# Attention's 64-row products in both array halves at once, on two-bank tiles

## The chip, the cores and the metric

The kernel runs on one core of a Trainium2 chip. The metric is the device time of one execution in microseconds. Before the change the median of three runs is 669.47 us (667.94 to 669.58).

A core has TensorE (matrix products, with a separate path that loads the stationary operand; PE and PEld in the profile), VectorE (DVE), ScalarE (ACT), GpSimd (POOL), and SyncE (SP), which here issues nearly all transfers. Products land in PSUM, eight banks of 512 float32 columns on 128 partitions. Each engine works its own list of instructions in order.

## The reference

One layer of a hybrid attention step over 128 context tokens and 1024 latent tokens of width 1024. After a modulated RMS norm, one projection gives queries, keys, values and gates of two mixers. Mixer A attends globally, mixer B within 128 positions, with a learned sink logit per head. Each has 8 query heads and 2 key heads of 64 dimensions.

```
q_a, k_a, v_a, g_a, q_b, k_b, v_b, g_b = project(h, w_in, ...)     # rmsnorm of q and k per head, rotary positions
o_a = softmax(q_a . [cached k, latent k] / 8) . [cached v, latent v]           # all 1152 keys
o_b = softmax over [sink, cached keys, latent keys with |i - j| <= 128] . v    # the sink has no value
x   = x + gate * (concat(o_a * silu(g_a), o_b * silu(g_b)) @ w_out)
```

Context tokens use the same weights and attend to themselves alone. Everything is float32. The kernel keeps that precision by writing each operand x as a rounded high part plus the low part that is left (x = hi + lo), and multiplying hi.hi, hi.lo and lo.hi.

## The kernel before, in words

Up to about 300 us the kernel normalises, projects and writes queries (high part in 64 rows, low part in the next 64) and gates to DRAM; keys and values stay on the core. The change leaves this part nearly as it is. The rest is attention.

**Units and pairs.** A unit is one query tile of 128 tokens, one mixer and one key head, so four query heads: 512 columns, head after head. There are 36: tiles 1 to 8 of latent tokens with four units each (A and B for key head 0, A and B for key head 1), then the context tile. Two units, an A and a B, form a pair; there are 18. An A unit has 9 blocks of 128 keys, a B unit 4 (3 at the first and last tile), a context unit 1.

**Maxima** (`max_steps`, `pmx`). To find each query's largest score, A multiplies each head's queries with 3 x 384 keys, 12 products a unit (L1111), each reduced on VectorE (L1124). B multiplies each head with its window, 4 products (L1114); VectorE adds the mask and takes the maximum with the sink in one custom instruction (L1129). The queries stand as high and low parts in 128 rows against the key's high part twice, so one product sums both. The negated maxima are transposed (L1168), copied on ScalarE (L1179), sent to DRAM (L1180), and come back as one row of the tile `qb` (L1184).

**Scores** (`score_steps`, `st`). For each block two products of 512 columns go into one bank: the key's high part against high and low queries (L1371, 128 rows), and 65 rows of the key's low part with a row of ones against the high queries and the row of negated maxima (L1372). At a B window's edges VectorE adds the mask (L1377). ScalarE takes the exponential into a `pe` tile (L1383). The `pe` tiles of a unit are added up (L1396): A's eight adds on GpSimd, B's three on VectorE.

**Burst** (`values`, `pv`). At the due time `v2` of a pair TensorE multiplies all `pe` tiles with the values, two products a block, one in each half of the output partitions (L1413); behind each unit's blocks come the products of the sum `acc` with ones, which give the softmax's denominator. Each is recorded as two matmuls. Then the ends: `t` adds the sink's weight (B, VectorE), `e` inverts by a logarithm and an exponential (ScalarE), `g` multiplies (VectorE), `o` applies the gate (GpSimd), `h` and `l` split into high and low parts (ScalarE, GpSimd).

**Output projection** (`out_items`, `po`). Each pair adds 24 products of 512 columns to its tile's two banks (L1488); when the tile's second pair is in, VectorE multiplies by the gate and adds the residual (L1495, L1496), and SP stores.

**Order.** Every step has a due time in the tables `STEPS` and `OTHER`, given per pair and shifted by `PAIR = 13` for each next one; LATE gives those of 24 gate products left over from the projection. `of_pair` posts the steps, and the loop at the end emits them by due time. `in_order` then ties each engine, SP too, to that order, so an engine never works ahead past a step that waits.

PSUM tiles: two banks A for maxima, two B for scores, two C for bursts, D and E for the output.

## Time and profile before

| What | us |
|---|---|
| Median of three runs (lowest, highest) | 669.47 (667.94, 669.58) |
| Span of the profiled execution | 667.9 |
| TensorE, its weight loads busy | 659.0, 519.3 |
| VectorE, ScalarE, GpSimd busy | 438.8, 281.6, 333.1 |
| Transfers | 81.41 MB, mean 122 GB/s |

The page gives no time for the profiled execution other than its span; the lowest run lies at 667.94, the median 1.6 above the span. A matmul's own duration in the groups, some 395 ns for 512 columns, includes its way through the array; how closely they follow one another is read from the chain, which gives each its share of time.

### The profile page before, as it was taken

What the parts mean: (1) busy time and instruction counts of PE and PEld (TensorE: products, weight loads), DVE (VectorE), ACT (ScalarE), POOL (GpSimd) and SP (SyncE); (2) the same over time, 40 slices, a digit from 0 to 9 for tenths busy, and PEclk for the clock granted to TensorE, in tenths of its full rate; (3) what the DMA queues carried; (4) which work ended last, traced back from release to release, by engine and by line L of the source; (5) the groups of instructions that cost most, each with busy time, mean ns of one, the idle gap of its engine ahead of it and who ended that gap; (6) DMA issues with size and microseconds to landing.
All of it is one profiled execution on the core that took longest, in us unless ns stands there. A gap on an engine that the chain in (4) does not pass through costs nothing.

```text
span 667.9 us, 10668 instructions
## 1 busy us (share of the span) xinstructions
PE 659.0 (99%) x3767; PEld 519.3 (78%) x3767; DVE 438.8 (66%) x923; ACT 281.6 (42%) x586; POOL 333.1 (50%) x325
## 2 busy tenths in 40 slices
PE   8999999999999999999999999999999999999997
PEld 3789988877788788997777777777777777777766
DVE  3566147786674866446768878688787786875533
ACT  4545411242141453435554355444454355434531
POOL 3457013332321332357885575657665675557712
PEclk9999999999999999999999999999999999999999
DMA  9970365437645310734142303223132212332233
GB/s 357 414 261 14 131 224 158 87 78 225 184 111 142 95 48 33 228 128 146 58 132 99 100 26 102 88 72 92 45 119 88 71 51 86 123 93 77 75 104 111
DMA packets 55837, 81.41 MB, mean 122 GB/s; under 512 B 7388, under 2 KB 26932, under 8 KB 54760
## 3 DMA queue, kind: packets, MB, share of 16 engines
q1 hardware_dynamic: 47464, 68.97, 30.8%
q10 hardware_dynamic: 8320, 11.77, 7.0%
q8 instruction: 30, 0.49, 0.3%
q14 instruction: 23, 0.19, 0.1%
HBM read 61.42 MB, written 19.29 MB: 121 GB/s over the span
## 4 chain that ended last, share of the span: by engine, by line
PE 92%; DVE 2%; ACT 2%; DMA 1%; issue 1%; ACTq 1%; POOL 0%; DVEq 0%
PE pv L1413 15%; PE po L1488 15%; PE st L1371 7%; PE st L1372 7%; PE pmx L1111 5%; PE pq L482 4%; PE pq L483 4%; PE pq L481 4%; PE pg L496 3%; PE pg L491 3%; PE pg L495 3%; PE pk L482 2%; PE pk L483 2%; PE pk L481 2%; PE pmx L1114 2%; PE px L645 1%
## 5 line engine op out<-in xcount | busy, mean ns | idle before, releaser
L1396 POOL TENSOR_TENSOR acc<-acc,pe 128x512 f32<-128x512 f32 x112 | 150.2, 1341 | 6.8 <-ACT pe L1383 0.6
L1383 ACT ACTIVATE pe<-st 128x512 f32<-128x512 f32 x208 | 120.6, 595 | 65.0 <-PE st L1372 52.2
L1124 DVE TENSOR_REDUCE mx<-pmx 128x1 f32<-128x384 f32 x192 | 104.5, 554 | 35.0 <-PE pmx L1111 32.2
L1413 PE MATMUL pv<-pe,v_all 128*64 128x256 f32 x832 | 96.8, 381 | 0.0
L1413 PEld LDWEIGHTS pv<-pe,v_all 128*64 128x64 f32 x832 | 58.2, 137 | 33.0 <-PE st L1372 4.2
L1488 PE MATMUL po<-wo,ogh 128*128 128x512 f32 (+1 forms) x224 | 79.3, 386 | 0.0
L399 POOL TENSOR_TENSOR rs_q<-ms_q,mhalf 128x8 f32<-128x8 f32 x18 | 34.8, 1932 | 80.4 <-DVE ms_q L397 80.4
L1111 PE MATMUL pmx<-kha,qt 128*128 128x384 f32 x192 | 64.2, 347 | 0.0
L1371 PE MATMUL st<-qt,kha 128*128 128x512 f32 x144 | 57.4, 399 | 0.5 <-ACT pe L1383 0.5
L1372 PE MATMUL st<-qb,kla 65*128 65x512 f32 x144 | 57.2, 397 | 0.0
L1129 DVE CUSTOM_DVE_ANT_0 pmx<-pmx,mask,nsink 128x512 f32<-128x512 f32 (+1 forms) x64 | 44.2, 722 | 11.3 <-PE pmx L1114 11.2
L1488 PEld LDWEIGHTS po<-wo,ogh 128*128 128x128 f32 x224 | 41.5, 189 | 9.6 <-ACT ogh L1450 0.6
L1445 POOL TENSOR_TENSOR spare<-spare,sgl 128x256 f32<-128x256 f32 x27 | 19.6, 737 | 49.9 <-DVE spare L1441 47.5
L1111 PEld LDWEIGHTS pmx<-kha,qt 128*128 128x128 f32 x192 | 35.3, 189 | 11.4 <-issue 5.0
L1488 PE MATMUL po<-wo,ogl 128*128 128x512 f32 (+1 forms) x112 | 43.2, 387 | 0.0
L664 POOL TENSOR_TENSOR h<-hf,h 128x256 fp32r<-128x256 f32 (+2 forms) x33 | 28.0, 863 | 21.3 <-DVE h L663 21.2
L1396 DVE TENSOR_TENSOR acc<-acc,pe 128x512 f32<-128x512 f32 x28 | 34.3, 1224 | 5.2 <-ACT pe L1383 3.9
L842 ACT ACTIVATE sqq<-pq 128x512 f32<-128x512 f32 x18 | 10.8, 600 | 53.3 <-DMA qd<-qo0q 15.2
L1371 PEld LDWEIGHTS st<-qt,kha 128*128 128x128 f32 x144 | 27.1, 189 | 5.6 <-ACT pe L1383 1.2
L495 PE MATMUL pg<-h,whigb 128*128 128x512 f32 (+2 forms) x88 | 30.0, 341 | 0.0
L1372 PEld LDWEIGHTS st<-qb,kla 65*128 65x128 f32 x144 | 27.0, 188 | 3.6
L496 PE MATMUL pg<-h,wlogb 128*128 128x512 f32 (+2 forms) x88 | 29.7, 337 | 0.0
(236 smaller groups left out, 1502.6 us busy)
## 6 DMA issues: line engine op xcount, KB each, us to landing
qt<-qd SPq DMA_DIRECT2D x36, 256.0 KB
wm<-in_w_mod_ss_dram SPq DMA_DIRECT2D x8, 1024.0 KB
qd<-qo0q ACTq DMA_DIRECT2D x36, 128.0 KB
qd<-qo1q ACTq DMA_DIRECT2D x36, 128.0 KB
qb<-qd SPq DMA_DIRECT2D x36, 128.0 KB
sgl<-gd SPq DMA_DIRECT2D x36, 128.0 KB
out_dram<-yt SPq DMA_DIRECT2D x17, 256.0 KB
wg<-in_w_mod_g_dram SPq DMA_DIRECT2D x4, 1024.0 KB
```

The costliest lines, as they stand in the source:

```text
L481: nc.tensor.matmul(out, h_at(0, i, k, tok), w.hi[k], start=(k == 0), stop=False)
L495: nc.tensor.matmul(out, w.hi[k][:, cs], h_at(0, i, k, to), start=(k == 0 and first), stop=False)
L496: nc.tensor.matmul(out, w.lo[k][:, cs], h_at(0, i, k, to), start=False, stop=False)
L1111: nc.tensor.matmul(pm[:, 0:384], lhs, kha[:, g, 3 * b : 3 * b + 3, :], start=True, stop=True)
L1124: nc.vector.tensor_reduce(mx[:, h, b : b + 1], pm[:, 0:384], axis=AX.X, op=ALU.max)
L1129: nc.vector.tensor_tensor_reduce(s, s, mask[:, m0 : m0 + P * (p1_ - p0)], -1.0, nsink[:, 4 * g + h : 4 * g + h + 1], op0=ALU.add, op1=ALU.min,
L1371: nc.tensor.matmul(s, kh, qtile[i], start=True, stop=False)
L1372: nc.tensor.matmul(s, kl, qbtile[i], start=False, stop=True)
L1383: nc.scalar.activation(pe, v["s"], AF.Exp)
L1396: (nc.vector if (m, b) in ADD_DVE else nc.gpsimd).tensor_tensor(acc[i], first, pe, op=ALU.add)
L1413: nc.tensor.matmul(pv[HD * s : HD * s + HD, o : o + 256].rearrange("p (c n) -> p c n", c=2), lhs, r[:, :, s, :], start=start, stop=stop)
L1488: nc.tensor.matmul(po[c], x, wo_parts[KT * n + k][lo][:, q], start=(k == KS[0] and p == 0), stop=(k == KS[-1] and p == 2))
```

## The change

The attention's TensorE work, bursts apart, is cut into products of 64 contraction rows. They are issued two by two: one uses rows 0 to 63 of the array, the other rows 64 to 127, and they write to two different banks.

- Queries are loaded so that the high part stands in both halves of `qt`, the low part in both halves of `qb` (`twice`, two transfers for each). The row of maxima is broadcast to 128 partitions, a tile `nm` of its own; a constant tile `part` of -1/64 turns it into "minus the maximum" by a product. Keys' low parts have 128 rows.
- Maxima take the high parts alone, two heads at once: an A unit has four pairs of products of 512 columns and two of 128, reduced from two banks in five reduces; a B unit has two pairs and two reduces. For B, ScalarE writes the mask into PSUM first and the products add to it. The first pair's two A units (`early`) keep their 12 products.
- Scores are made for two key blocks at once in a two-bank tile, four products in each half: hi.hi, hi.lo, lo.hi and the maxima. At a window's edges ScalarE writes the mask first. One exponential takes both banks. A's ninth block is cut by heads, 256 columns in each half.
- The output projection multiplies 64 rows at a time, one half into each of the tile's two banks, and the halves swapped for 12 of a pair's 24 steps; the context tile's keeps 128 rows.
- PSUM becomes two tiles S of two banks (scores and part of the maxima), one tile C of two banks (both units' burst, the other maxima), D and E. A's maxima use S, C, S, C, C; B's use C, C.
- The burst holds both units' values; a plain product among them transposes the next pair's maxima. The products with ones stand behind both units' values, as a step `vs`.
- Of B's three adds the first two move to GpSimd (`ADD_DVE`).
- All due times are new: `STEPS` for even pairs, `ODD` for odd ones, `OTHER` for seven pairs.

The order that the new due times give on TensorE around a burst, in two neighbouring pairs in the middle: burst, ones-products, 4 or 7 output products, one or two of B's score groups, B's first maximum, then output products, A's score groups and maxima by turns, with the last A group shortly ahead of the next burst. GpSimd's order is: the two gatings `o`, B's adds (in every second pair one of them among A's), the low parts `l`, and A's eight adds.

```diff
+PE2 = 7
+PE1 = 2
...
-ADD_DVE = ((1, 1), (1, 2), (1, 3))
+QBS = 2
+ADD_DVE = ((1, 3),)
...
+TURN_AT = 4
+MAX_AT = ("SCSCC", "CC")
+PRE = ()
...
-    kla = kv.tile([65, 2, 9, P], F32R, name="kla")
+    kla = kv.tile([P, 2, 9, P], F32R, name="kla")
...
+    part = kv.tile([P, P], F32R, name="part")
+    nc.vector.tensor_scalar(part.rearrange("p (a n) -> p a n", a=2), ones.unsqueeze(1).to_broadcast([P, 2, HD]),
+                            -1.0 / HD, None, op0=ALU.mult)
...
+    def twice(to, src):
+        for s in range(2):
+            nc.sync.dma_start(to[HD * s : HD * s + HD].bitcast(F32), src)
+
+    HALF = (slice(0, HD), slice(HD, P))
...
-        nc.sync.dma_start(qt_.bitcast(F32), q_dram[t][m][:, 512 * g : 512 * g + 512])
+        twice(qt_, q_dram[t][m][0:HD, 512 * g : 512 * g + 512])
...
+        def masked(k):
+            p0, p1_ = cut(k)
+            v[k] = pair_of_banks(MAX_AT[1][k], f"pmx{i}_{k}")
...
+            nc.scalar.copy(v[k][:, :, 0:w], mask[:, m0 : m0 + w].unsqueeze(1).to_broadcast([P, 2, w]))
...
+                p0, p1_ = cut(k)
+                w = P * (p1_ - p0)
+                if m == 0:
+                    v[k] = pair_of_banks(MAX_AT[0][k], f"pmx{i}_{k}")
+                for a, h in enumerate((k,) if m else (0, 1) if k == 4 else (k // 2,)):
+                    for s, half in enumerate(HALF):
+                        at = P * (2 * h + s)
+                        nc.tensor.matmul(v[k][:, s, w * a : w * a + w], q[half, at : at + P],
+                                         (khb if m else kha)[half, g, p0:p1_, :], start=m == 0 and a == 0, stop=True,
+                                         skip_group_check=m == 1 or a > 0)
 
...
+            elif m == 0 and k == 4:
+                nc.vector.tensor_reduce(mx[:, :, 2].rearrange("p (a s) -> p s a", s=2),
+                                        pm[:, :, 0 : 2 * P].rearrange("p s (a n) -> p s a n", a=2), axis=AX.X, op=ALU.max)
...
+                h, b = divmod(k, 2)
+                nc.vector.tensor_reduce(mx[:, 2 * h : 2 * h + 2, b], pm, axis=AX.X, op=ALU.max)
...
-                nc.vector.tensor_tensor_reduce(s, s, mask[:, m0 : m0 + P * (p1_ - p0)], -1.0,
-                                               nsink[:, 4 * g + h : 4 * g + h + 1], op0=ALU.add, op1=ALU.min,
-                                               accum_out=mx[:, h : h + 1])
+                p0, p1_ = cut(k)
+                nc.vector.tensor_reduce(mx[:, 2 * k : 2 * k + 2], pm[:, :, 0 : P * (p1_ - p0)], axis=AX.X, op=ALU.max)
...
-            qb_ = qp.tile([65, 512], F32R, tag="qb", name=f"qb{i}", bufs=QBS)
-            nc.sync.dma_start(qb_[0:64, :].bitcast(F32), q_dram[t][m][0:64, 512 * g : 512 * g + 512])
+            qb_ = qp.tile([P, 512], F32R, tag="qb", name=f"qb{i}", bufs=QBS)
+            twice(qb_, q_dram[t][m][HD:P, 512 * g : 512 * g + 512])
...
-            nc.sync.dma_start(qbtile[i][64:65, :].bitcast(F32),
-                              r_dram[i // 2][4 * m : 4 * m + 4].rearrange("(o h) n -> o (h n)", o=1))
+            nmtile[i] = qp.tile([P, 512], F32R, tag="nm", name=f"nm{i}", bufs=2)
+            nc.sync.dma_start(nmtile[i].bitcast(F32),
+                              r_dram[i // 2][4 * m : 4 * m + 4].rearrange("(o h) n -> o (h n)", o=1).to_broadcast([P, 512]))
...
+    def pair_of_banks(tag, name):
+        return ps2.tile([P, 2, 512], F32, tag=tag, name=name, bufs={"S": 2, "C": 1}[tag])
...
+            def before(j=j, two=two, edge=edge, v=v):
+                v["s"] = pair_of_banks("S", f"st{i}_{j}")
...
+                if edge:
+                    x = x.rearrange("p s (h n) -> p s h n", n=P)
+                    k = mask.rearrange("p (s n) -> p s n", n=P)
+                    k = (k[:, 0::3].unsqueeze(2).to_broadcast([P, 2, 4, P]) if two else
+                         k[:, 3 if t == NL else 0].unsqueeze(1).unsqueeze(1).to_broadcast([P, 2, 2, P]))
+                    nc.scalar.copy(x, k)
...
+            def product(j=j, blks=blks, two=two, edge=edge, pre=pre, v=v):
+                assert i in rowed
+                if not pre:
+                    v["s"] = pair_of_banks("S", f"st{i}_{j}")
+                qh, ql = qtile[i], qbtile[i]
+                last = 3 if edge or not pre else 2
+                for n in range(last + 1):
+                    for s, half in enumerate(HALF):
+                        kh, kl = blks[s if two else 0][0:2]
+                        k, q = ((kh, qh), (kh, ql), (kl, qh), (part, nmtile[i]))[n]
+                        to = v["s"][:, s] if two else v["s"][:, s, 0:256]
+                        nc.tensor.matmul(to, k[half], q[half, :] if two else q[half, 256 * s : 256 * s + 256],
+                                         start=n == 0 and not pre, stop=n == last, skip_group_check=pre)
...
+            def weights(j=j, blks=blks, two=two, v=v):
+                if two:
+                    pe = w3.tile([P, 2, 512], F32, tag="pe2", name=f"pe{i}_{j}", bufs=PE2)
+                    nc.scalar.activation(pe, v["s"], AF.Exp)
+                    v["pe"] = [pe[:, 0], pe[:, 1]]
+                else:
+                    pe = w3.tile([P, 512], F32, tag="pe1", name=f"pe{i}_{j}", bufs=PE1)
+                    nc.scalar.activation(pe.rearrange("p (s n) -> p s n", s=2), v["s"][:, :, 0:256], AF.Exp)
+                    v["pe"] = [pe]
...
-        n = len(made)
-        for b, (blk, pe) in enumerate(made):
-            product(0, blk[1], pe, first and b == 0, False)
-        if not last:
-            return
-        product(256, ones, acc.pop(i), False, True)
+        for b, (lhs, pe) in enumerate(made):
+            if b == (min(at, len(made) - 1) if then else -1):
+                then()
+            product(0, lhs, pe, b == 0, False)
...
+        def halves(r, k, p):
+
+            for s, half in enumerate(HALF):
+                c = (r + s) % 2
+                first = k == KS[0] and p == 0 and r == 0
+                if first:
+                    po[c] = one_bank(pieces[c][2], f"po{t}_{c}")
+                oh, ol = (x[half, k % 2, :] for x in og[t, k // 2])
+                x, lo = ((oh, 0), (oh, 1), (ol, 0))[p]
+                nc.tensor.matmul(po[c], x, wo_parts[KT * c + k][lo][half], start=first,
+                                 stop=k == KS[-1] and p == 2 and r == 0, skip_group_check=True)
...
-        mms = [lambda c=c, k=k, p=p: mm(c, k, p) for c in range(len(pieces)) for k in ks for p in range(3)]
+        if last:
+            mms = [lambda c=c, k=k, p=p: mm(c, k, p) for c in range(len(pieces)) for k in ks for p in range(3)]
+        else:
+            mms = [lambda r=r, k=k, p=p: halves(r, k, p) for r in (g, 1 - g) for k in ks for p in range(3)]
...
+    def burst(i):
+
+        pvt = pair_of_banks("C", f"pv{i}")
+        u = i // 2 + 1
+
+        def turned():
+            if 2 * u < NU:
+                rowpt[u] = pvt[0:12, 1, 0:P]
+                nc.tensor.matmul(pvt[0:HD, 1, 0:P], m_all[u % 2].bitcast(F32), ident_r.bitcast(F32), start=True, stop=True)
+
+        values(i - 1, pvt, TURN_AT, turned)
+        if u in puts_:
+            puts_[u]()
+        values(i, pvt)
+
+    def burst_sums(i):
+
+        for j in (i - 1, i):
+            assert added.get(j, 0) == sum(len(blks) for blks, _ in held_[j]) - 1
+            sums[j]()
 ```

## Prediction

> **What bounds the kernel now.** I read the page's busy times first, then its chain, then two steady stretches of the attention part, then the chain in order of time there, and last the groups of instructions between 330 and 640 us. Engines and shares of the whole span:
>
> ```profile
> PE 659.0 (99%) x3767; PEld 519.3 (78%) x3767; DVE 438.8 (66%) x923; ACT 281.6 (42%) x586; POOL 333.1 (50%) x325
> PEclk9999999999999999999999999999999999999999
> PE 92%; DVE 2%; ACT 2%; DMA 1%; issue 1%; ACTq 1%; POOL 0%; DVEq 0%
> 375.29:396.94 21.65, 21.65 (x129) 16.49 (x131) 15.82 (x32) 10.12 (x21) 13.56 (x14) 1.00 0.21 68
> 396.94:418.59 21.65, 21.65 (x129) 16.49 (x131) 18.14 (x36) 10.11 (x21) 13.56 (x14) 1.00 0.28 92
> ```
>
> TensorE holds 92% of the chain at full clock. The last two lines are one pair of units each (PE, PEld, DVE, ACT, POOL busy us): PE is busy for all of it, VectorE for 16 to 18, GpSimd for 13.6. So TensorE's issue sets 21.65 us a pair. Its prices, from the chain in order of time (start, us, what):
>
> ```profile
> 331.36 0.35 PE pmx L1111 x2
> 332.91 6.19 PE pv L1413 x56
> 375.29 6.62 PE pv L1413 x60
> 381.91 0.54 PE pmx L1111 x2
> 382.45 1.16 PE po L1488 x5
> 383.62 0.23 PE st L1371
> 383.85 0.23 PE st L1372
> 390.72 0.24 PE st L1372
> 390.95 0.47 PE pmx L1114 x2
> 396.94 6.62 PE pv L1413 x60
> 591.61 6.62 PE pv L1413 x60
> 650.48 1.95 PE pv L1413 x16
> ```
>
> A 512-column product costs 0.235 (0.231 in `po`), a 384-column one 0.175; a burst costs 6.62 for 60, 0.110 each. Check: scores 26 x 0.235 = 6.11, maxima 12 x 0.175 + 4 x 0.235 = 3.04, burst 6.62, output 24 x 0.231 = 5.54, 0.19 for leaving the burst (0.54 against 0.35), 0.1 for a transpose: 21.6.
>
> **The change on TensorE.** Call p the price of two 64-row products, one in each array half, 512 columns. No row shows one. The nearest is the burst, whose products stand in two column halves: two cost 0.221. The other end is today's 0.235 for one full product; I take 0.228, since both the columns and today's form are kept. In such slots a pair has: A's scores 4 groups x 4 + one half-wide group = 18, B's 8, output 24, so **none of these loses a slot**; A's maxima 4 and two of 128 columns, about 4.5, instead of 12 full products; B's maxima 2 instead of 4. That is 56.5 p. Burst 6.62, leaving it 0.19, and the transpose, now a plain product inside the burst, at most one slot (0.22): 7.03 more. PE per pair: 56.5 x 0.221 + 7.03 = 19.5 to 56.5 x 0.235 + 7.03 = 20.3, so 1.3 to 2.1 less, nearly all from the maxima. The 24 late gate products keep 128 rows, in three clusters by their due times: six changes of form, 6 x 0.1 = 0.6 us once.
>
> The Trainium skill, "TensorEngine Tiling (Array Packing)", section "Tiling Modes" (Key Properties), says that changing the tiling mode drains TensorE. The 0.54 against 0.35 agrees. By this rule the output projection is cut in halves for the mode, not for speed; left at 128 rows among the scores, each of its some 10 clusters a pair would cost two drains, 10 x 0.19 = 1.9 us by the row, and the maxima's gain would be gone.
>
> **The change on the other engines.** Groups between 330 and 640 us (busy us, mean ns), and GpSimd in order of time:
>
> ```profile
> L1396 POOL TENSOR_TENSOR acc<-acc,pe 128x512 f32<-128x512 f32 x102 | 137.0, 1343 | 5.8
> L1456 POOL TENSOR_TENSOR ogl<-of,ogh 128x256 fp32r<-128x256 f32 x7 | 5.1, 733 | 3.6 <-ACT ogh L1450 3.6
> L1158 POOL TENSOR_TENSOR m_all<-m_all,sink 128x4 f32<-128x4 f32 x16 | 3.2, 203 | 21.8 <-DVE m L1150 18.2 <-DMA er<-rd 3.3
> 383.82 0.73 POOL L1445 TENSOR_TENSOR of<-of,sgl 128x256 f32<-128x256 f32 x1 [5.65 <-DVE of L1441]
> 384.51 0.74 POOL L1445 TENSOR_TENSOR spare<-spare,sgl 128x256 f32<-128x256 f32 x1
> 387.86 4.04 POOL L1396 TENSOR_TENSOR acc<-acc,pe 128x512 f32<-128x512 f32 x3
> 391.85 0.75 POOL L1456 TENSOR_TENSOR ogl<-spare,ogh 128x256 fp32r<-128x256 f32 x1
> L1383 ACT ACTIVATE pe<-st 128x512 f32<-128x512 f32 x182 | 105.6, 595 | 59.1 <-PE st L1372 46.7 <-DVE st L1377 9.5
> L1434 ACT ACTIVATE rs<-rs 128x256 f32<-128x256 f32 x30 | 12.5, 417 | 1.0
> L1433 ACT ACTIVATE rs<-rs 128x256 f32<-128x256 f32 x15 | 6.3, 418 | 25.0 <-DVE rs L1428 25.0
> L1450 ACT CAST ogh<-spare 128x256 fp32r<-128x256 f32 x22 | 8.8, 398 | 0.0
> L1244 ACT CAST wo_big<-wraw 128x512 fp32r<-128x512 f32 x1 | 0.6, 611 | 0.0
> L1124 DVE TENSOR_REDUCE mx<-pmx 128x1 f32<-128x384 f32 x156 | 84.7, 553 | 19.2 <-PE pmx L1111 16.6
> L1122 DVE TENSOR_REDUCE mx<-pmx 128x4 f32<-128x512 f32 x4 | 2.7, 680 | 0.0
> L1396 DVE TENSOR_TENSOR acc<-acc,pe 128x512 f32<-128x512 f32 x27 | 33.2, 1228 | 5.2 <-ACT pe L1383 3.9
> L1496 DVE TENSOR_TENSOR yt<-po,yt 128x512 f32<-128x512 f32 x14 | 9.7, 692 | 0.5
> L1441 DVE TENSOR_TENSOR of<-pv,rs 128x256 f32<-128x256 f32 x8 | 3.4, 425 | 3.4 <-ACT rs L1434 3.4
> L1428 DVE TENSOR_TENSOR rs<-pv,er 128x256 f32<-128x256 f32 x15 | 6.4, 424 | 6.9 <-PE pv L1413 6.9
> ```
>
> ScalarE: no row has 1024 columns. Bounds: 0.595 (no price for more columns) and 1.19 (two of today's). From 256 to 512 columns it goes from 0.40 to 0.60, so 0.2 for 256 and about 1.0 for 1024. A pair then has six exponentials at 1.0 and one at 0.6, and three masks written to PSUM at 1.0: with 1.67 for the inverses, 0.8 for casts and 0.46 of small ones 12.5, against 10.1. Room in 20.
>
> VectorE: 128 columns more cost 0.127, so a two-bank reduce about 1.2 (bounds 0.68 and 2 x 0.68). Six of them, one of 512, one add and the ends make some 12 against 16 to 18: the masks' adds, the fused mask-and-maximum and two of B's three adds go. VectorE gets room.
>
> A tile's two output banks now fill together, so their sums on VectorE (2 x 2 x 0.69 = 2.8) come at once, and the next tile's first output product waits for them. Two or three score groups stand between, 1.9 to 2.8: 0 to 0.9 every second pair, in the waits below.
>
> GpSimd gets what VectorE loses: B's first two adds. Three in a row took 4.04, 1.35 each; the eight of A are 10.8, the two of B 2.7.
>
> DMA and its queue (issue ns as least, median, most; waits in us, times, longest):
>
> ```profile
> L1135 SPq DMA_DIRECT2D qb<-qd x36: 451/476/1112, 283.0 to 642.1; - x36
> L1184 SPq DMA_DIRECT2D qb<-rd x36: 220/244/433, 287.3 to 643.1; - x36
> SPq L1180 <- ACT spare L1179: 142.1, 17, 13.1
> ```
>
> The query halves come twice and the row of maxima goes to 128 partitions: 2 x (128 + 256) KB a pair, some 37 GB/s on 68 to 92. SP issues one `qt` and one `qb` more a unit and a broader row, 2 x (2 x 0.48 + 0.24) = 2.4 us a pair. SP stood 142.1 us, 8.4 a pair, behind the copy of the transposed maxima, so there is room. That copy moves into the burst; behind its wait on SP stand the rows of maxima that the next scores need. They have the rest of the burst, about 4.9 us, for two trips through DRAM; no row here times one trip. I take it as hidden; uncovered, up to 1 us a pair.
>
> **What is late next.** The two ones-products now stand behind both units' values, and need A's last add on GpSimd. By the due times GpSimd then does: both gatings, B's two adds, both low halves, the small sink step, A's eight adds. That closes a ring, from A's last add to A's last add of the next pair:
>
> - ones-products, 8 x 0.110: 0.9
> - total, two inverse steps, multiplication: 0.424 + 0.418 + 0.417 + 0.425, and 0.3 for handing over (estimate): 2.0
> - gatings 1.43, low halves 1.45, sink step 0.2: 3.1
> - B's adds 2.7, A's adds 10.8: 13.5
> - waits for exponentials and casts. After the ends (2.0) ScalarE first writes a mask into the freed tile (1.0) and only then takes B's first exponential (1.0), ready at 4.0, while GpSimd is there at 2.0 + 1.4 = 3.4: 0.6; a cast or A's first exponential alike: 1.4 in all. Bounds 0 and 2.8.
>
> Sum 20.9; 19.5 to 22.3 with its bounds. It is longer than PE's 19.5 to 20.3, so **GpSimd's ring becomes the bound**, and of the 1.3 to 2.1 us won on TensorE 21.65 - 20.9 = 0.75 is left. It now has no such ring to close: POOL idles 8 of 21.65.
>
> From the second burst (332.91) to the fourteenth (591.61) are twelve periods: 12 x 0.75 = 9.0. Ahead of it two units keep their twelve products, B's maxima lose 8 and the stretch's VectorE work shrinks: 2 won, 0.6 lost. From the fourteenth burst to the last (650.48) are 58.9 us, four periods of 14.7: the two full ones have no more than 20.9 to lose, the prompt's little to add: 0 to 2 lost, and the last output products, still 128 rows, stay; 1 won by half the maxima. Net 10.5. Profiled span 667.9 less 10.5 is 657.4; the runs' median, 669.47, is 1.6 above that span, the lowest run equals it. Forecast: **659**.
>
> **Rivals.** *TensorE stays the bound*: the ring's waits vanish because the schedule puts other work there. For it: 19.5 is the ring's own lower end. Gain 1.3 to 2.1 over some 14 pairs, 18 to 29: about 646 (640 to 651). Chance 0.2.
>
> *Slower: the one two-bank tile C.* It carries the burst of both units, both B maxima and three of A's. Place: ahead of B's first maximum after a burst. Price: burst 6.84, ends 2.0, B's maxima 2 x (mask 1.0 + 0.23 + 1.2), A's 2 x (0.23 + 1.2) + 0.8, and a wait for TensorE's last columns, about 0.2, six times: 18.6. It decides once its seven hand-overs lose over 0.44 each, (21.65 - 18.6) / 7; at 0.55 it is 22.45, 14 x 0.8 = 11 more: 680. Against it: much of that loss is room the engines have. Chance 0.14. The same page of the Trainium skill, section "Performance Considerations" (PSUM Bottleneck), warns that tiling speeds TensorE but not PSUM evacuation; the trace of before shows no such wait.
>
> *No change*: the ring takes its upper waits, 21.6: 668 to 670. Chance 0.1.
>
> *The halves do not work side by side.* Each slot then costs 0.47, 56.5 x 0.235 = 13 more a pair, some 200: 870. Only the column halves speak against it. Chance 0.03.
>
> **How the numbers follow.** Forecast 0.53 (its own range 652 to 666), the rivals 0.2, 0.14, 0.1, 0.03. A measurement can tell some 0.3%, 2 us. Faster: 0.53 + 0.2 = 0.73; same 0.1; slower 0.17. Range 644 to 674: it leaves out the fastest of the first rival and most of the slow ones.
>
> **What would show it.** Right: periods between bursts of 20.5 to 21.2; TensorE idle ahead of the ones-products, released by POOL `acc`, some 0.5 us a pair; two products starting within 0.01 us and the next two 0.22 to 0.235 later; POOL near 17 us a pair. Wrong: idle time ahead of B's maxima released by ScalarE (tile C), periods below 20.3 with no wait on `acc`, or slots of 0.3 and more.

## The result, and the profile after

The changed kernel takes 696.98 us (median of 4 runs, 696.4 to 698.48), the kernel before 668.86 (4 runs, 667.94 to 669.58) on the same chip. The ratio is 1.0422, with a 95% interval of 1.0403 to 1.044: 28 us slower, where 659 was forecast and 674 was the upper end. The profiled execution is the slowest of the four (698.48 us), so its spans are some 1.5 us above the median run's.

The page of the profiled execution (span 696.7): busy times, TensorE's clock and the chain's engines.

```profile
PE 662.0 (95%) x4684; PEld 513.0 (74%) x4684; DVE 370.3 (53%) x653; ACT 310.2 (45%) x542; POOL 370.2 (53%) x358
PEclk9999999999999999998999999999999999999999
PE 77%; DMA 12%; ACT 4%; DVE 2%; SPq 2%; issue 1%; ACTq 1%; POOL 0%; DVEq 0%
```

TensorE held 92% of the chain before and holds 77% now; transfers went from 1% to 12%. Where the 28.8 us of span lie can be read from the bursts of value products: the second and the fourteenth, from the chain in order of time (start, us, what).

```profile
340.60 1.95 PE pv L1414 x16
606.85 1.88 PE pv L1414 x16
```

The second starts 7.7 later than before (332.91). The twelve periods to the fourteenth take 266.25 (258.70): 7.6 lost. From there to the end 89.85 (76.3): 13.5. Two pairs in the middle, as stretches (span, then PE, PEld, DVE, ACT, POOL busy):

```profile
385.24:406.97 21.73, 20.79 (x184) 15.26 (x186) 11.39 (x14) 12.77 (x20) 15.96 (x16) 1.00 0.39 117
406.97:429.62 22.65, 21.56 (x185) 15.59 (x186) 14.07 (x18) 11.55 (x18) 16.28 (x16) 1.00 0.45 135
```

In both TensorE is idle for 0.9 to 1.1 us; before it was for none. In the twelve periods this makes 12.4 us (253.83 busy of 266.25).

For the steady pairs I added up, from the starts of all matmuls in the trace, each one's time until the next starts:

| us a pair | scores | maxima | output | burst with transpose | sum |
|---|---|---|---|---|---|
| before | 6.19 | 3.26 | 5.56 | 6.63 | 21.6 |
| after | 6.84 | 1.92 | 5.86 | 7.54 | 22.2 |

The maxima won 1.3, as forecast. The rest lost 1.9, though it has no more slots but the transpose. What the losses are shows in the products' waits from 300 us on (us in all, times, longest), and in SP's from 380 to 607:

```profile
PE st L1384 <- DMA nm<-rd: 11.8, 12, 2.2
PE pv L1414 <- ACT spare L1133: 6.1, 17, 0.4
PE pmx L1067 <- DMA qt<-qd: 1.7, 6, 0.5
```

```profile
SPq L1134 <- ACT spare L1133: 58.5, 10, 7.6
```

Scores wait for the row of maxima (`nm`): 3.4 us ahead of the second burst, 5.2 in the twelve periods (7 times), 3.1 behind them; a burst's value products wait for ScalarE's copy of the transposed maxima; maxima wait for queries, which stand on SP behind the write that waits for the same copy (before, SP stood 101.1 us behind its copy in such a window, and no product waited for queries). Behind the fourteenth burst scores also wait 1.9 us for queries. GpSimd's `acc`, the bound that was forecast, is not among them. The way of the row in one pair, from the chain:

```profile
387.11 0.10 PE pv L1552
387.22 2.30 PE pv L1414 x19
...
389.54 0.26 ACT spare L1133
...
389.82 1.27 DMA rd<-spare
...
391.14 3.87 DMA nm<-rd
...
395.06 1.43 PE st L1384 x10
```

The transposing product (L1552) is done at 387.2, but the copy starts 2.3 us later, at 389.54: it is released by the last of A's value products, which write to the same tile. Then the write takes 1.3 and the load to 128 partitions 3.9. From the product's start to the first use of the row are 7.9 us. TensorE's other work fills most of them: in this pair it stands 0.36 us ahead of the value products that wait for the copy and 0.58 ahead of the product that needs the row.

### The profile page after: what moved, and what is told of

Read it like the earlier page. It is cut to its first block, busy times and chain, and to the rows that moved or that the text cites. A ratio compares the mean times of both kernels' runs of the same rounds, so it can differ in the third digit from the quotient of the medians.

```text
span 696.7 us, 12252 instructions
## 1 busy us (share of the span) xinstructions
PE 662.0 (95%) x4684; PEld 513.0 (74%) x4684; DVE 370.3 (53%) x653; ACT 310.2 (45%) x542; POOL 370.2 (53%) x358
## 4 chain that ended last, share of the span: by engine, by line
PE 77%; DMA 12%; ACT 4%; DVE 2%; SPq 2%; issue 1%; ACTq 1%; POOL 0%; DVEq 0%
PE st L1384 13%; PE pv L1414 10%; PE po L1502 10%; DMA nm<-rd 7%; PE pq L411 4%; PE pq L412 4%; PE pq L410 4%; PE pmx L1067 4%; PE pg L420 3%; PE pg L424 3%; PE pg L425 3%; DMA rd<-spare 2%; PE pk L411 2%; PE pk L412 2%; PE pk L410 2%; DMA qt<-qd 2%
## 5 line engine op out<-in xcount | busy, mean ns | idle before, releaser
L1414 PE MATMUL pv<-pe,v_all 128*64 128x256 f32 x832 | 101.1, 384 | 6.2 <-ACT spare L1133 6.1
L1390 ACT ACTIVATE pe<-st 128x1024 f32<-128x1024 f32 x92 | 92.8, 1025 | 21.0 <-PE st L1384 18.3
L1502 PE MATMUL po<-wo,ogh 64*128 64x512 f32 x384 | 97.2, 404 | 0.0
L1414 PEld LDWEIGHTS pv<-pe,v_all 128*64 128x64 f32 x832 | 64.0, 136 | 35.2 <-ACT spare L1133 13.9
L1085 DVE TENSOR_REDUCE mx<-pmx 128x2 f32<-128x1024 f32 x56 | 67.8, 1221 | 14.8 <-PE pmx L1067 14.5
L1384 PE MATMUL st<-nm,part 64*128 64x512 f32 (+1 forms) x232 | 49.0, 388 | 11.8 <-DMA nm<-rd 11.8
L1088 DVE TENSOR_REDUCE mx<-pmx 128x2 f32<-128x1024 f32 (+1 forms) x32 | 37.0, 1156 | 39.0 <-PE pmx L1067 37.6
L1502 PEld LDWEIGHTS po<-wo,ogh 64*128 64x128 f32 x384 | 50.7, 187 | 7.0 <-issue 1.9
L1502 PE MATMUL po<-wo,ogl 64*128 64x512 f32 x192 | 53.3, 396 | 0.0
L1502 PE MATMUL po<-wo_big,ogh 64*128 64x512 f32 x128 | 48.2, 412 | 0.0
L1343 POOL TENSOR_TENSOR acc<-pe 128x512 f32<-128x512 f32 x28 | 36.2, 1293 | 21.9 <-ACT pe L1390 21.8
L1384 PEld LDWEIGHTS st<-nm,part 64*128 64x128 f32 x232 | 25.5, 188 | 21.7 <-DMA nm<-rd 18.4
L1042 ACT CAST pmx<-mask 128x1024 f32<-128x1024 bf16 (+1 forms) x32 | 30.8, 963 | 12.8 <-DVE mx L1088 6.6
L1384 PE MATMUL st<-qt,kha 64*128 64x512 f32 (+1 forms) x160 | 33.8, 391 | 0.9 <-ACT pe L1394 0.4
L1067 PE MATMUL pmx<-kha,qt 64*128 64x512 f32 (+1 forms) x168 | 31.1, 357 | 2.5 <-DMA qt<-qd 1.7
L1384 PE MATMUL st<-qb,kha 64*128 64x512 f32 (+1 forms) x160 | 32.8, 376 | 0.0
```

Of the source, the lines that this page charges most:

```text
L1067: nc.tensor.matmul(v[k][:, s, w * a : w * a + w], q[half, at : at + P], (khb if m else kha)[half, g, p0:p1_, :], start=m == 0 and a == 0, ...
L1085: nc.vector.tensor_reduce(mx[:, 2 * h : 2 * h + 2, b], pm, axis=AX.X, op=ALU.max)
L1088: nc.vector.tensor_reduce(mx[:, 2 * k : 2 * k + 2], pm[:, :, 0 : P * (p1_ - p0)], axis=AX.X, op=ALU.max)
L1343: (nc.vector if (m, b) in ADD_DVE else nc.gpsimd).tensor_tensor(acc[i], first if b == 1 else acc[i], x, op=ALU.add)
L1384: nc.tensor.matmul(to, k[half], q[half, :] if two else q[half, 256 * s : 256 * s + 256], start=n == 0 and not pre, stop=n == last, skip_gr ...
L1390: nc.scalar.activation(pe, v["s"], AF.Exp)
```

## The experiments

**Is it the row, or the queries queued behind it?** Theory R: the row's way. Rival Q: SP's queue. Rival C: tile C or GpSimd's adds hold the pair anyhow.

`e1_copy_early`, the copy written down right behind the product:

```diff
-        values(i - 1, pvt, TURN_AT, turned)
-        if u in puts_:
-            puts_[u]()
+        def turned_and_put():
+            turned()
+            if u in puts_:
+                puts_[u]()
+        values(i - 1, pvt, TURN_AT, turned_and_put)
```

> One call moved: ScalarE's copy of the transposed maxima is written down right behind the transposing product, ahead of the rest of A's value products; same instructions, same queues. Theory R (the way of the row of maxima: product, copy, write, broadcast load, first scores, too long for the work that TensorE has left): in the changed kernel the copy starts 2.4 us after the product, when A's last value product signals. With the call moved it should start within 0.4 us, B's value products should lose their 0.5 us a pair, and the waits of the scores for the row (30 us in 31 waits, most of 2 us or less) should nearly go: 696.7 - 17 x 0.5 - some 20 = 668 (660 to 676). Rival Q (not the row, but the query loads queued on SP behind the write that waits for the copy): these start 2.2 us sooner too, and only the waits of the maxima for the queries go, 0.4 us a pair beside the 0.5: 681 (678 to 686). Rival C (the one tile of two banks C, or GpSimd's adds, hold the pair at 22.2): only the place of the wait changes, 693 to 697.

Measured: 686.69 (ratio to before 1.0279, 1.0255 to 1.0303), 10.3 better than the changed kernel, little more than a third of what R expected and nearer to Q's 681; the waits below and e3 decide between them. R's 30 us add the weight loads' waits for the row (18.4) to the products' (11.8), which are largely the same time twice. ScalarE's copy in order of time (start, us; last, in brackets, the idle time before it and what ended it), the products' waits from 300 us on, and the chain after a burst:

```profile
404.05 0.25 ACT L1133 COPY spare<-pv 12x128 f32<-12x128 f32 x1 [1.37 <-PE pv L1552]
```

```profile
PE pmx L1067 <- ACT pmx L1042: 7.2, 14, 0.7
PE pv L1414 <- ACT spare L1133: 6.3, 17, 0.8
PE st L1384 <- DMA nm<-rd: 1.7, 2, 1.5
```

```profile
411.97 1.03 ACT pmx L1042
412.99 0.04 issue
413.04 0.54 PE pmx L1067 x2
...
413.67 1.24 DVE mx L1088
414.91 0.02 issue
414.93 1.02 ACT pmx L1042
415.95 0.96 ACT pe L1390
416.91 0.04 issue
416.95 1.21 PE st L1384 x8
```

The copy is now released by the product itself. The waits for the row fell from 11.8 to 1.7, but two others hold: A's next value product now waits for the copy, since both touch one tile, and B's maxima wait for ScalarE's mask. That is the turn of tile C: ends, mask, product, reduce, second mask, and a score group's exponential behind it on ScalarE. Periods are 21.6 and 22.3 by turns, the shorter no better than the 21.65 of before.

`e2_two_rows`, `e3_write_on_scalar`, `e4_old_row`:

```diff
 e2:
-            nc.sync.dma_start(nmtile[i].bitcast(F32), ... .to_broadcast([P, 512]))
+            nc.sync.dma_start(nmtile[i].bitcast(F32)[0::HD], ... .to_broadcast([2, 512]))
...
+                        rows_ = half if n < 3 else slice(HD * s, HD * s + 1)
...
 e3, e4:
-            nc.sync.dma_start(r_dram[u][a:b], rw)
+            (nc.scalar if u else nc.sync).dma_start(r_dram[u][a:b], rw)
 e4:
-                              r_dram[i // 2][4 * m : 4 * m + 4]...
+                              r_dram[max(i // 2 - 1, 0)][4 * m : 4 * m + 4]...
...
-                    nc.scalar.activation(pe, v["s"], AF.Exp)
+                    nc.scalar.activation(pe, v["s"], AF.Exp, scale=0.25)
```

> The row of maxima is loaded to 2 partitions (0 and 64) instead of 128, and its product takes one contraction row in each half instead of 64; the sum is the same. Copy, write and queue are as in the changed kernel. Theory R: the load takes 3.9 us from issue to landing in the changed kernel, 128 times 2 KB; with two rows it should land in some 2 us, which takes off most of the 30 us that scores wait for the row: 680 (674 to 686), while B's value products still wait 0.5 us a pair. Rival Q: the query loads stand as late as before, 692 to 697. Rival C: 694 to 697.

> The write of the transposed maxima to DRAM is issued by ScalarE's queue, right behind its copy, instead of SP's; so SP no longer stands behind the copy, and the query loads behind it go out earlier. Rival Q: the waits of the maxima for the queries go (about 0.4 us a pair in the steady part, 14 pairs) and the start and the end of the stretch gain as much: 684 (680 to 689). Theory R: copy, write and load of the row stay as late as they are, so the waits of the scores stay: 690 to 697. Rival C: 694 to 697.

> Leaves out the dependence on the pair's own maxima: the row is loaded from the pair before (same load, same bytes, same product), the write goes out on ScalarE's queue, and the exponentials are scaled by 0.25 so that they stay finite; the output is not the reference's. Nothing then waits for the way from the transposing product to the row but the sink's weights. Theory R: the waits of the scores for the row go, those of B's value products for the copy (0.5 us a pair) stay: 674 (668 to 682). Rival C: another wait takes the place, 692 to 697. Rival Q: as in the run with the write on ScalarE, 680 to 689.

Measured: e3 695.03, 2.0 better, so Q falls: with SP free of the copy the maxima's waits for queries shrink (0.4 in one), but the row's stay (12.0 us in 9 waits). e4, which leaves out each pair's own row and so does not compute the reference, takes 683.3, 13.7 better: that much is won with the row's way gone and the write on ScalarE's queue, and then the mask's wait (7.1) and the copy's (6.1) stand as in e1. e2 722.41, 25 worse than the changed kernel, though its row came in time. The weight loads' waits of e2:

```profile
PEld st L1385 <- issue: 39.4, 112, 0.7
PEld st L1385 <- DMA nm<-rd: 1.1, 2, 0.8
```

The smaller load did what R said; but 112 times a score product now waits 0.35 us for nothing that the trace names, where the changed kernel has none of note: the one-row products stand between 64-row ones, and I take it as the price of a change of form, which g0 below bears out.

**What is left?** Theory W: two independent waits. Theory G: GpSimd's ring. `e5_turn_in_s` and its variants:

```diff
 e5, on e1:
+                tt = pair_of_banks("S", f"tt{u}")[:, 0] if u < NU // 2 - 1 else pvt[:, 1]
+        d["sa"] = d["sa"][:4] + (max(d["sa"][4], DUE[u - 1]["po"][11] - PAIR + 0.001),)
 e6, on e5:
-            nc.scalar.copy(v[k][:, :, 0:w], mask[:, m0 : m0 + w].unsqueeze(1).to_broadcast([P, 2, w]))
 e7, on e5:
+    d["nx"] = (the due time of the third output product behind it, ...)
 e8, on e5:
-ADD_DVE = ((1, 3),)
+ADD_DVE = ((1, 1), (1, 2), (1, 3))
```

> As the run with the copy moved, but the transposing product writes to a free tile S instead of B's bank of the burst's tile, so no value product shares a tile with what ScalarE copies (the last transpose of all stays where it was). So that the output products of both row halves into one bank stay ordered, the last A score group, half a group, is placed behind the neighbouring output products, ahead of the burst. Theory W (what is left after the row's way are two waits of their own: 0.56 us a pair of the value products behind the copy, and some 0.75 a pair of B's maxima for ScalarE's mask in tile C): the first goes, 17 x 0.56 = 9.5 off 686.7: 677 (673 to 681). Theory G (GpSimd's adds in a ring with the ones-products, the forecast's own bound, 20.9 a pair or a little more, hold the pair now): the wait reappears ahead of the ones-products: 683 to 687.

> As the run with the transpose in tile S, but the masks that ScalarE writes ahead of B's maxima are left out (no work in their place; the products start the banks afresh), so B's maxima also run over keys outside the window. Theory W: the wait of B's maxima for the mask, 0.75 us a pair in the run with the copy moved, goes with 2 us of ScalarE's work a pair: 677 - 14 x 0.75 = 666 (662 to 671). Theory G: the ring stays: within 3 us of the run with the transpose in tile S.

> As the run with the transpose in tile S, but B's first maximum is placed three output products later in TensorE's list in pairs 2 to 15 (three slots, 0.7 us); masks, reduces and queues stay. Theory W: the same 0.75 us a pair is then filled with output products: 667 (663 to 672), nearly as without the masks. Rival: tile C's turn (burst, ends, mask, B's first maximum, reduce, second mask) is itself the bound, so the wait only moves to B's second maximum or the next burst: 675 to 680.

> As the run with the transpose in tile S, but all three of B's adds are on VectorE again, so GpSimd has 2.6 us a pair less. Theory G: the ring loses 2 x 1.31 us, and the period falls by what the ring holds: 10 us or more faster than with the transpose in tile S, below 670. Theory W: GpSimd has 16 us of work in a pair of 22 and no ring closes: within 2 us of the run with the transpose in tile S, 675 to 680.

Measured: e5 690.45, e6 682.0, e7 694.95, e8 698.07. All four missed W's numbers, for a reason that e5's own edit brings in:

```profile
PE st L1392 <- DVE mx L1093: 9.7, 6, 1.6
```

The moved score group came behind the mask of the next pair's edge tile, got the other tile S, and waited for a reduce in every second pair (e5's periods: 21.65 and 23.1). Within the four, e6 is 8.5 below e5: the masks cost that. In e7 the steady periods are e5's to 0.1 us but for one, so nothing was filled, as its rival said; with the artefact in both, it tests no more than that. In e8 VectorE's reduces are late instead (5.2 us of waits for them), and nothing is won; e5's products wait for GpSimd's adds only once, 0.2 us, so no ring holds there.

With the edge mask behind the transpose (f2), and three versions on that: f1 lets VectorE add B's mask again, f3 is f1 with e3's write on ScalarE's queue, f4 is f2 with the edits of e6 and e3.

```diff
 f2, on e5:
+    d["pb"] = tuple(max(x, DUE[u - 1]["v2"] - PAIR + 0.0005) for x in d["pb"])
 f1, on f2, beside the mask's line of e6:
-                nc.vector.tensor_reduce(mx[:, 2 * k : 2 * k + 2], pm[...], axis=AX.X, op=ALU.max)
+                    nc.vector.tensor_tensor_reduce(pm[:, s, 0:w], pm[:, s, 0:w], mask[:, m0 : m0 + w], 1.0,
+                                                   sink[...], op0=ALU.add, op1=ALU.max, accum_out=mx[:, h : h + 1])
```

> As the run with the transpose in tile S, but the mask that ScalarE writes into a score tile S for the next pair's B edge is placed behind the burst's transpose in every pair. In that run it stood ahead of the last A score group in every second pair, so that this group got the tile whose reduce was late, and TensorE stood 2 us (every second period 23.1 instead of some 21.2). Theory T (the turn of the one tile C, burst, ends, mask, B's first maximum, reduce, second mask, is the bound once the row comes early): the artefact goes, 6 x 1.9 = 11 off 690.5, and the periods stay near 21.5: 679 (676 to 683). Theory W (tile C's waits can be filled by TensorE): 668 (664 to 672).

> As the run with the edge mask later, but B's maxima get their mask as in the kernel before: VectorE adds it and takes the maximum in one custom instruction per head (0.76 + 0.14 us), ScalarE writes no mask for them. Theory T: two masks of 1.0 leave tile C's turn and VectorE takes 2 x (2 x 0.9 - 1.2) = 1.2 more in it, and ScalarE's exponentials no longer stand behind the second mask: 0.9 to 1.3 us a pair, 14 pairs: 665 (661 to 670). Theory G (GpSimd's ring): no change against the run with the edge mask later, within 2 us.

> As the run with the fused mask, but the write of the transposed maxima is issued by ScalarE's queue. Theory R (way of the row): in the steady part nothing changes; in the last three pairs, which have little other work, the loads of the row stand on SP behind that write and behind two query loads, 2.6 us, so 2 to 4 us at the end: 662 (658 to 667). Rival (the end is bound by its products and ends): within 1 us of the run with the fused mask.

> Leaves out the masks ahead of B's maxima as in the run without them (so the maxima also run over keys outside the window), with the edge mask later and the write on ScalarE's queue. Bound of what the mask's place can give: all three waits gone. Theory T: periods of 20.5, as in the undisturbed pairs of the run without masks: 661 (657 to 665), 2 to 4 below the run with fused masks and write. Theory G: periods stay at 21 or more: 670.

Measured: f2 680.8, as T said: against e1 5.9 less, which I take as the price of the copy's tile: the waits for the copy fell from 6.3 to 0.4 (f2 also moves one score group and the edge's mask). f1 675.57 (1.0111, 1.0095 to 1.0126): 5.2 less, where some 14 were expected. f3 676.84, no gain where 662 was expected. f4, which leaves out the masks ahead of B's maxima, 672.09 (1.0053, 1.0033 to 1.0073), beyond G's 670 and far from T's 661. Stretches of f4 (two pairs, then the twelve periods from its second burst), and the first of its weight loads' waits:

```profile
420.80:441.10 20.30, 20.30 (x184) 15.91 (x182) 11.37 (x14) 10.14 (x16) 15.85 (x16) 1.00 0.35 99
441.10:462.30 21.20, 20.92 (x184) 15.63 (x182) 13.61 (x18) 10.15 (x16) 16.32 (x16) 1.00 0.46 144
337.89:587.27 249.38, 247.72 (x2182) 190.79 (x2184) 148.94 (x181) 122.82 (x194) 196.73 (x184) 1.00 0.43 125
```

```profile
PEld pv L1424 <- POOL acc L1353: 6.9, 14, 0.8
```

With the three waits gone, TensorE is busy for all of every second period, 20.3 us, and the twelve periods take 249.4 against 258.7: 9.3 won. The ones-products now wait for GpSimd's adds, as they did in f2 (8.8 us of weight loads' waits there, 16 times). In the longer period shown, from the last value product ahead of them (446.78) to the first of them it is 0.66 us instead of 0.11, so the adds make some 0.55 of the 0.9 by which the longer period exceeds the shorter. f1, which computes all of the reference, takes 253.9 for the twelve periods, 4.8 less than before, and loses 3.3 ahead of them and 7.4 behind. In f4 the second burst still comes 5.0 us later than before (337.89 against 332.91), and the rest takes 82.5 against 76.3.

**The start, the end, and the change of form.** g1 transposes the last pair's maxima a burst earlier; g2 adds to it the first write on ScalarE's queue and the first four gate loads behind the first rows; g3 adds to that a later place for the output sums; g0 is the changed kernel with 128-row output products; h1 is f4 and h2 is g2 without g1's edit, both with A's fourth add on VectorE.

```diff
 g1, on f3:
+                out += [("tt", j, lambda: (last_turn(i // 2), put(j)))]
...
 g2, on g1:
-        load_gate(i)
+        post(zero[0] - 40.0, lambda i=i: load_gate(i))
...
 g3, on g2:
+        d["ym"], d["ys"] = (-7.34, -7.36), (d["ys"][0], -7.33)
 g0, on the changed kernel:
-        if last:
+        if True:
             mms = [lambda c=c, k=k, p=p: mm(c, k, p) ...]
 h1, h2:
-ADD_DVE = ((1, 3),)
+ADD_DVE = ((1, 3), (0, 4))
```

> As the run with fused mask and write on ScalarE, but the last pair's maxima are transposed (into a tile S), copied and written right behind the burst before the last but one, and its rows are loaded as soon as the tiles are free, instead of from inside the last but one burst. Theory E (the end still pays the way of the row once in full: product at 643.3, first scores at 650.5 in the run without masks, with 3.4 us of other work): 4 to 5 us less, 672 (670 to 674). Rival: the end is bound by burst, ends and the last 45 output products; the wait only moves: 675 to 677.

> As the run with the last turn early, and at the start of the attention the first pair's maxima are written by ScalarE's queue too and the first four gate loads stand behind the first rows on SP, instead of ahead of them. Theory F (the start loses its 3 us against the kernel before because the write stands behind twelve issues on SP of half a us each, with the row's load behind it): first burst at some 312.5 instead of 315, 2 to 3 us less: 669.5 (668 to 672). Rival (landing itself, 3 us behind 1 MB of other loads, is the bound): within 1 us of the run before it.

> As the run with the front changed, but in pairs 3 to 13 the two output banks' sums (2.8 us on VectorE, every second pair) stand behind B's second fused maximum instead of ahead of it, and the next tile's first three output products behind the scores that follow. Theory V (in the run with fused masks every second period is 22.0 instead of 20.4 since B's second maximum waits 0.8 us for VectorE, and the rest for GpSimd's adds): five to six pairs lose 0.8 us less: 666 (664 to 669). Rival G (GpSimd's ring then takes it back): within 1.5 us of the run with the front changed.

> The changed kernel with its output projection left at 128 rows in all tiles: the same 24 products a pair at the same places in the list. It prices the change of the array's form: by the forecast's step some 10 clusters a pair, two changes each at 0.1 us from the row that leaves a burst (0.19 for both): 1.9 us a pair, 16 pairs: 30 us on top of 697, less what the waits for the row of maxima cover: 715 (705 to 727). Rival (a change of form costs nothing beside what the waits have already): 695 to 700.

> As the run without masks and with the write on ScalarE's queue (masks of B's maxima left out), but the fourth of A's eight adds moves from GpSimd to VectorE. Theory G (with the three waits gone, what is left in every second period, 21.2 instead of 20.3, is GpSimd's ring of the forecast: the ones-products wait for A's last add): the ring loses 1.3 us, these periods fall to some 20.4, 6 x 0.8 = 5: 667 (665 to 670), and the waits of the ones-products for the adds are gone. Rival (VectorE's add delays reduces or ends as in the run with B's adds on VectorE): 671 to 678, with waits for VectorE.

> A version that computes the whole reference: the run with the front changed, without its early last turn, and with the fourth of A's adds on VectorE. Theory G: from 675.5, five to six periods of 22.0 lose what they wait for the adds, some 0.6 each: 672 (669 to 675). Rival (VectorE, which has the fused masks here, is late in these periods): 675 to 680.

Measured: g1 679.37 (675.89 to 680.59), no gain: in f3 the scores wait only 0.4 us for rows from 380 us on, so there was next to none to win, and the moved transposing product itself waits 2.0 us for VectorE. g2 675.53 (1.0113, 1.0096 to 1.013), 3.8 below g1 but only 1.3 below f3, where 669.5 was expected; its first burst starts at 314.4, between f3's 315.1 and the expected 312.5. g3 687.95; in one pair its sums stand behind the next tile's first products and take those in place of their own, with as much work; elsewhere every second period is 23.4 to 24.9, and output products wait 11.4 us for the sums: a miss, which does not tell whether VectorE's order was a loss in g2. h1 683.87 and h2 684.31, outside all that was expected. In h1 no burst waits for GpSimd any more, but

```profile
PE pv L1424 <- DVE mx L1095: 6.1, 6, 1.1
```

VectorE's add waits for GpSimd's third, and A's last reduces stand behind it. So whether the ring alone holds f4's 21.2 stays open; that the wait for the adds is there, and that the two moves of work off GpSimd (e8, h1) cost more elsewhere, is shown. No version beats the kernel before.

g0 took 745.42 (1.1157, 1.113 to 1.1183): 48 more than the changed kernel. Of its weight loads' waits from 300 to 697 us, one that is 0.4 us, once, in the changed kernel, whose output projection keeps 128 rows for the context tile alone:

```profile
PEld po L1490 <- issue: 33.4, 105, 0.7
```

On the way back, score products wait 19.8 us in 61 such waits (1.3 in 4 in the changed kernel). A steady pair takes 25.4 instead of 22.2; with 17.6 changes between output and 64-row products in it, 0.18 us each.

## Why the prediction was wrong, step by step

- **Slots and p: right.** All three kinds of products run side by side. Two halves start together and the next two 0.23 later, from TensorE in order of time (x2 stands for two products):

```profile
400.97 0.40 PE L1384 MATMUL st<-qt,kha 64*128 64x512 f32 x2
401.21 0.40 PE L1384 MATMUL st<-qb,kha 64*128 64x512 f32 x2
```

p is 0.233, near the upper bound of 0.235 and not the 0.228 taken. PE is 20.3 where nothing waits (f4), the upper bound too.

- **Prices on the other engines: right.** Exponential, reduce and mask, from the groups of the page (count, busy us, mean ns):

```profile
L1390 ACT ACTIVATE pe<-st 128x1024 f32<-128x1024 f32 x92 | 92.8, 1025 | 21.0 <-PE st L1384 18.3
L1085 DVE TENSOR_REDUCE mx<-pmx 128x2 f32<-128x1024 f32 x56 | 67.8, 1221 | 14.8 <-PE pmx L1067 14.5
L1042 ACT CAST pmx<-mask 128x1024 f32<-128x1024 bf16 (+1 forms) x32 | 30.8, 963 | 12.8 <-DVE mx L1088 6.6
```

- **"I take it as hidden; uncovered, up to 1 us a pair": this is the step that failed.** The step put the term at nothing, judging the row's way by two transfers against 4.9 us. The copy begins 2.3 us late, since it is released by A's last value product; write and load take 5.2 more. Without dependence on the row the kernel takes 683.3 (e4): 13.7 of the 28. The two profiles are 15.6 apart: 5.2 ahead of the second burst, 3.8 in the twelve periods, 6.6 behind them. So in a steady pair the price, 0.3 us, is within the step's own "up to 1 us"; the larger part lies where the step did not look. The twelve periods, which miss the forecast by 16.6 (9.0 won, 7.6 lost), do so for several causes in turn: 266.2 us become 262.7 with the copy early (e1), 259.2 with it out of the tile (f2), 253.9 with fused masks (f1) and 249.4 with none (f4). At the start and the end pairs have little other work, and there the forecast had 1.4 won and a change of 1 us or less, where 7.7 and 13.5 were lost. The last pair's rows (chain):

```profile
670.02 0.25 PE pv L1552
...
673.37 4.00 DMA nm<-rd
...
677.42 0.38 PE st L1384 x2
```

These are 7.4 us from product to scores. Other products fill all but 1.0 of them (TensorE is busy for 6.15 of the 7.15 us from 670.27 to 677.42), so this pair alone is not the end's loss: behind the fourteenth burst scores wait 3.1 us for rows in three places and 1.9 for queries.

- **"The transpose ... at most one slot (0.22)": too low.** The product costs no more than that, but its copy holds value products of the same tile, 0.4 a pair (6.1 us in 17 waits); out of the tile 5.9 us are won (e1 to f2).
- **Tile C, the slower rival: its chance of 0.14 was too small.** The place is as described (idle ahead of B's maxima, released by ScalarE), and e1's shorter period, 21.6, is what the forecast's hand-overs of 0.44 would make; the hand-overs themselves were not timed. But it is a later layer: in the changed kernel B's maxima wait only 0.9 us for masks, in e1 7.2, once the row comes early, and there the masks cost 5 to 9 us (f2 to f1 and f4, e5 to e6).
- **The ring as bound: wrong for the changed kernel.** There no product waits for `acc`. With three other waits gone (f4) the wait that was named is there, in every second period. That f4's twelve periods win 9.3 where 9.0 was forecast, at 20.8 on average where 20.9 was, is luck: they are 20.3 and 21.2 by turns, and f4 leaves out a mask that the forecast's ring counted.
- **The change of form.** The rule of the Trainium skill, "TensorEngine Tiling (Array Packing)", section "Tiling Modes", that a change drains TensorE, agrees with g0 and, as far as I read it rightly, e2. The forecast's 1.9 us a pair for 128-row output products was low: 3.2.
- **Open:** what makes the rest of the loss at the start and the end. f4 still has 5.0 and 6.2 of it. At the start a half clock (last section) lasts from 313.3 to 320.1 us in f4, worth at most some 3 us, and h2's second burst is only 0.9 late; which of its edits did that is not shown. Of the end no run took away more than a part.

## What to carry to other kernels

Before a step is called hidden, follow its result hop by hop to the first instruction that needs it: which instruction signals it, what shares its tile, how long each transfer lands, what stands ahead in each queue; and do so once for a steady pair and once for the first and the last. When several waits stand behind one another, taking away the longest pays only up to the next: here 21 to 25 of the 28 us were three layers (10, 6 and 5 to 9), and a ledger of single experiments showed the third where the changed kernel's profile had only 0.9 us of waits for it.

## What the runs showed of the hardware that was not expected

TensorE's granted clock was halved after idle times that are shorter than I had thought harmful. In the changed kernel it is idle from 323.9 to 326.06, and then (2 us each; PE busy behind the span, the clock third from the end):

```profile
324.00:326.00 2.00, 0.00 (x0) 0.00 (x0) 1.44 (x4) 1.05 (x3) 0.77 (x2) 1.00 0.85 248
326.00:328.00 2.00, 1.55 (x8) 0.85 (x9) 1.12 (x1) 1.45 (x3) 1.13 (x2) 0.60 1.02 265
...
332.00:334.00 2.00, 2.00 (x16) 1.91 (x14) 0.00 (x0) 1.47 (x3) 1.20 (x3) 0.69 0.00 0
```

Half clock lasts 6.8 us here and 3.4 after an idle time of 1.94 at 661.6; after one of 2.03 at 483.0 it does not come. In e1 it came for 3.4 us after 1.47 (at 312.3), in f1 not after 1.73 (at 312.3), so the length alone does not decide. The two cost at most some 5 us of TensorE's work (half of 6.8 and of 3.4), which a wait's own length does not show. The mean granted clock is 0.989 to 0.994 in the changed kernel's four runs and 0.998 to 1.0 in e4's, so some of e4's 13.7 us may come this way. The Trainium skill, "TensorE: Matmul & The Clock Gate", section "HAM oscillation — how this bites in real kernels", warns of gaps beyond some 3.4 us; by these traces 1.5 to 2 can be enough.
